# Opening the weight rooms' pool first, token 512 in other psum banks and on GpSimd, and a gate's Silu made earlier, in a fused Fourier and Hyena encoder layer

## The chip, the cores and the metric

The kernel runs on one core of a Trainium2 chip. The metric is device time in microseconds (us) of one launch, both sequences together. TensorE (PE) does the matmuls and the transposes; VectorE (DVE), ScalarE (ACT) and GpSimd (POOL) do elementwise work; SyncE (SP) and GpSimd's queue issue the transfers between HBM and the on-chip memory (SBUF). Matmul results land in psum banks.

## The reference, cut to what matters

Two sequences of 1024 tokens and 1024 channels go through one encoder layer, each as a batch of one. In the kernel they are batch row 0 and batch row 1.

```python
xn = rmsnorm(x, g_pre)
p = xn @ w_in                          # sections fv, fg, hv (three), hg, mg
fv, fg, hv, hg, mg = jnp.split(p, ...)

fz = fftn(fv by groups of 256 channels, axes=(tokens, channels), norm="ortho").real
y_f = (fz * silu(fg)) @ w_fourier_out

v, x1, x2 = jnp.split(short_conv(hv, w_short), 3, axis=-1)
z = v
for n, gate in enumerate((x1, x2)):
    z = gate * long_conv(z, filter spectrum n, hyena_d[n])
y_h = (z * silu(hg)) @ w_hyena_out

g_f, g_h = sigmoid(mg + b_merge) in two halves
out = (g_f * y_f + g_h * y_h) @ w_out
return x + rmsnorm(out, g_post)
```

The filters come from a small sine network: taps are made, weighted by an exponential decay, normalised, and transformed to spectra. In the kernel's numbering of w_in's sections 0 is fg, 1 to 3 are v, x1 and x2, 4 is hg, and 5 and 6 are mg. All values are fp32; every matmul operand is split in a high part `h` and a low part `l`, and three products are added (`mm3`).

## The kernel before

Four phases follow one another.

1. The Fourier phase, up to about 211 us with a tail to 250. Per 128 channels `xtile` (L334) transposes and scales x (`tpx`, tile `xg`), and forms sums and differences of tokens (`eo`, split to `eh` and `el`); token 512 has no partner and goes to a small tile `x5` (L360 and L361, two instructions of 128x2 for each k and batch row). The values fv (`pfv`) are computed in halves of 512 channels in the order (0,0), (0,1), (1,1), (1,0) of (batch row, half). In each half token 512 gets a product of its own, `pfx`, 16 matmuls into the psum tile `p5` (L410); its copy `x5t` enters the token stage (`stage`, psum `pse` and `pso`, copied to `sev`). A channel stage follows (`pP`, `pQ`, tiles `fPs`, `fPm`, `fA`, `fB`), and its result is stored to `d_fz` by GpSimd's queue. Psum has tags of a few banks each: "mm" of 4 banks, "T" of 2 and "X" of 2. The token stage uses "T" or "X".
2. `phase_main`, up to about 700 us. It makes 16 filter spectra: taps (psum `pft`, tiles `T`, `ex`, `acc`), their norm (`pn`), a butterfly and a transform (`pXf`, with the tables `cfw0` and `cfwd`). Between them stand 30 in-projections of gates for batch row 0 (`spill_gate`): sections 5 and 6 with eight tiles each, six tiles of section 4, and eight of section 0. A spilled gate goes to `d_g` in HBM. Section 0 gets its Silu there, as ps x (1 + tanh(ps / 2)) / 2, since tanh shares an ACT table with exp; the others are copied as they are.
3. The branches (`branches`), up to about 1640 us: short convolution, transform (`tph`, `pX`), product with the spectra and inverse transform (`pT`, tile `y`, cast to `yh`, remainder `yl`) for eight channel tiles, two orders and two batch rows. For section 4 of batch row 0 the first six tiles (`early`) load their gate from `d_g`, take Silu on ACT (L1021) and GpSimd multiplies; tiles 6 and 7 project the gate there.
4. The output blocks, up to 2408 us, in an order that is written out by hand.

An in-projection (`inproj`, L751) of a 128 x 1024 output tile is 48 matmuls of 128x512. Its weight comes in two halves. Each half needs a room of a high and a low tile: SP loads `wr`, ACT casts it to the high part (L773), ACT writes the negative of that to the low part (L774), and GpSimd's queue adds the original weight in HBM to it (an accumulating DMA, L775). Rooms go round in turns of four: two pairs `wh` and `wl`, then `draw` in the constant pool, then `draw2`, which has 4096 bytes per partition in the pool `m2`. The tile of the last two is called `whl`.

Up to the blocks the instruction order on each engine is not written by hand. A scheduler simulates the program with costs of its own and lets an instruction go when its operands, its tile and its psum bank are free in that simulation; each engine then runs its list strictly in order. A tile pool takes the address range that is free when it is opened, so the order of pools in `phase_main` decides which tiles of the Fourier phase a room or a table must wait for.

Of the kernel before, what the change touches and what calls it, by code (L numbers as in the profile page):

```python
# [12 lines left out]
AF = mybir.ActivationFunctionType  # L13
ALU = mybir.AluOpType
MUL, ADD, SUB = ALU.mult, ALU.add, ALU.subtract
# [146 lines left out]
class K:  # L162
# [171 lines left out]
    def xtile(self, b, k, px, fo):  # L334


        nc, a = self.nc, self.a
        if b == 0:
            xk = lambda m: self.xs[m][:, k * P:(k + 1) * P]
        else:  # L340
            xt = px.tile([P, 8, P], F32, tag="x", name=f"xk{b}_{k}", bufs=3)
            nc.sync.dma_start(xt, a[f"x{b}"].rearrange("(m p) c -> p m c", p=P)[:, :, k * P:(k + 1) * P])
            xk = lambda m: xt[:, m]
        xg = px.tile([P, L + 2], F32, tag="xg", name=f"xg{b}_{k}", bufs=2)
        nc.gpsimd.memset(xg[:, L:L + 2], 0.0)
        for n in range(2):
            tp = self.psum("mm", 4, "tpx") if b else self.psum("T", 2, "tpx")
            for q in range(4):
                m = 4 * n + q
                self.mm(tp[:, q * P:(q + 1) * P], xk(m), self.diag[:, m], True, True)  # L350
            nc.scalar.activation(xg[:, 512 * n:512 * n + 512], tp, AF.Copy, scale=self.gpre[:, k:k + 1])
        self.stored = nc.sync.dma_start(self.d_x[b][k], xg[:, 0:L])
        eo = px.tile([P, 2, 2, 256], F32, tag="eo", name="eo", bufs=2)
        fw = xg[:, 0:512].rearrange("p (a r) -> p r a", r=2)
        bw = xg[:, 1024:512:-1].rearrange("p (a r) -> p r a", r=2)
        self.add("dve", eo[:, 0], fw, bw)
        self.sub("pool" if b else "dve", eo[:, 1], fw, bw)
        self.split(fo["eh"][:, k], fo["el"][:, k], eo, "dve", "act")
        x5 = fo["x5"][:, k]
        mid = xg[:, 512:513].to_broadcast([P, 2])  # L360
        self.split(x5[:, b:b + 33:32], x5[:, 2 + b:35 + b:32], mid, "dve" if b else "pool", "dve" if b else "pool")  # L361


    def open_weights(self, pw):
# [26 lines left out]
    def fourier_half(self, b, half, W, fo, px, pf, begun={}):  # L391

        nc = self.nc
# [5 lines left out]
        for e, (W_, n, X_) in enumerate(((WE, 260, EE), (WO, 256, OO))):  # L399
            for m in range(4):  # L400
                p = begun.get((e, m))
                if p is None:
                    p = self.psum("mm", 4, f"pfv{e}")
                    for k in range(8):
                        self.pfv(p, e, m, k, W, fo)
                self.split(X_[0][:, m], X_[1][:, m], p[:, :n], "dve", "act")
                if e == (b + half == 0):

                    if m == 0:
                        p5 = self.psum("X", 2, "pfx")[0:36, :260]  # L410
                    for k in (2 * m, 2 * m + 1):
                        for i in range(2):
                            self.mm(p5, fo["x5"][:, k], WE[i][:, k], k + i == 0, k + i == 8)
# [390 lines left out]
    def spill_gate(self, b, sec, ct, ws):  # L804


        nc = self.nc
        ps = self.inproj(sec, ct, plain=b > 0)
        for n in range(2):
            s = slice(512 * n, 512 * n + 512)  # L810
            t = self.wp.tile([P, 512], F32, tag="gt", name="gt", bufs=3)
            if sec:
                nc.scalar.copy(t, ps[n])
            else:
                f = self.wp.tile([P, 512], F32, tag="gt", name="fz", bufs=3)
                nc.sync.dma_start(f, self.d_fz[b][ct][:, s])
                nc.scalar.activation(t, ps[n], AF.Tanh, scale=0.5)
                self.stt("dve", t, t, 1.0, ps[n], ADD, MUL)
                self.stt("dve", t, t, 0.5, f, MUL, MUL)
            nc.sync.dma_start(self.d_g[b][sec][ct][:, s], t)  # L820
# [92 lines left out]
    def phase_main(self, nct=8, nb=NB, nf=16):  # L913
        tc, nc, a = self.tc, self.nc, self.a
        with ExitStack() as es:
            pool = lambda n: es.enter_context(tc.tile_pool(name=n, bufs=1, reuse_waits="tile"))
            mf, wa, wb, mi = pool("mf"), pool("wa"), pool("wb"), pool("mi")
            self.stage2 = pool("m2")
            self.turn, self.unsaved = 3, []
            ws = Rooms(wa, wb)  # L920
            self.load_x(0, range(4))
            self.hid = ws.tile([P, L], F32R, tag="q", name="hid", bufs=2)
            hid = ws.tile([P, L], F32, tag="q", name="hidr", bufs=2)
            nc.sync.dma_start(hid, self.d_h)
            nc.scalar.copy(self.hid, hid)
            self.sub("dve", self.hid[64:128], hid[64:128], self.hid[64:128])
            taps = self.filter_taps(0, 0, ws)
            self.load_x(0, range(4, 8))
            self.cfw0 = mf.tile([P, 4 * P], F32, name="cfw0")
            self.cfwd = mf.tile([P, 2, 12 * P], F32R, name="cfwd")  # L930
            nc.sync.dma_start(self.cfw0, a["c_fw0"])
            nc.gpsimd.tensor_copy(self.cfwd[:, 0, 0:1], self.xl[4][:, 0:1])
            nc.gpsimd.dma_start(self.cfwd, a["c_fwd"])
            for t, n in ((self.th, "c_th"), (self.wsh, "w_short"), (self.bm, "b_merge")):
                nc.sync.dma_start(t, a[n])
            plain = [(5, c) for c in range(8)] + [(6, c) for c in range(8)] + [(4, c) for c in range(NH)]
            fill = sorted([((2 * c + 1) / len(plain), t) for c, t in enumerate(plain)]
                          + [((2 * c + 1) / max(NF, 1), (0, c)) for c in range(NF)])
            fill = [t for _, t in fill]
            for i in range(nf):  # L940
                nxt = self.filter_taps((i + 1) % 2, (i + 1) // 2, ws) if i + 1 < nf else None
                gates = fill[i * len(fill) // nf:(i + 1) * len(fill) // nf]
                if i < nf - 1:
                    self.filter_spectrum(i % 2, i // 2, taps, ws)
                for sec, c in gates:
                    self.spill_gate(0, sec, c, ws)
                if i == nf - 1:
                    first = [self.conv(1 + n, 0, ws, "vx"[n], 0, True) for n in range(2)]
                    self.filter_spectrum(i % 2, i // 2, taps, ws)
                taps = nxt  # L950
                if i == 4:
                    self.cinv = mi.tile([P, 2, INVW], F32R, name="cinv")
                if 4 <= i < 12:
                    w = slice((i - 4) * INVW // 8, (i - 3) * INVW // 8)
                    with tc.issue_after(self.added.ins):
                        nc.gpsimd.dma_start(self.cinv[:, :, w], a["c_inv"][:, :, w])
            self.branches(nb, nct, ws, *first)
# [33 lines left out]
    def branches(self, nb, nct, ws, v0, x0):  # L991
# [3 lines left out]
        tc, nc = self.tc, self.nc  # L995
# [8 lines left out]
        Z, X = {}, {}  # L1004
# [6 lines left out]
        def gates(i):  # L1011
            b, n, c = steps[i]
            x = self.conv(2 + n, c, ws, f"x{n + 1}", b)
            if n and b == 0:
                early = c < NH
                ps = None if early else self.inproj(4, c)
                for q in range(2):
                    sg = self.wp.tile([P, 512], F32, tag="gt", name="sg", bufs=3)
                    if early:
                        nc.sync.dma_start(sg, self.d_g[0][4][c][:, 512 * q:512 * q + 512])  # L1020
                    nc.scalar.activation(sg, sg if early else ps[q], AF.Silu)  # L1021
                    self.mul("pool", x[:, 512 * q:512 * q + 512], x[:, 512 * q:512 * q + 512], sg)
            X[i] = x
        B = self.conv_front(v0, ws)
# [509 lines left out]
```

## Time and profile before

| what | value |
|---|---|
| median of three runs | 2417.44 us (2414.99 to 2423.45) |
| the profiled execution | 2422.64 us, span 2420.8 us |
| PE busy | 2360.9 us, 98% of the span, 13006 matmuls |
| DVE busy | 1978.2 us, 82% |
| ACT busy | 1147.2 us, 47% |
| GpSimd busy | 460.4 us, 19% |
| moved by DMA | 499.37 MB |
| mean granted PE clock | 0.993 |

A row of a timeline has the start, the length of the whole group, engine, line, operation, output and input tiles, and shape; x16 are sixteen such instructions in a row. In brackets stands how long the engine idled before it and what it then got. L194 is the helper through which nearly all matmuls are issued and L181, L177, L173 and L171 are helpers for elementwise work, so groups are told apart by their tiles. Busy matmuls overlap: a 128x512 matmul is shown with about 0.39 us, though one can start every 0.23 us. A row of the waits has the engine with what it was to run, the releaser, and then the total, the count and the longest.

### The profile page before, as it was taken

To read this page: it belongs to the slowest core of one execution; us is meant where nothing else is said; L and a number is where in the kernel's file an instruction comes from. 1 tells how busy PE (TensorE), PEld (TensorE's weight loads), DVE (VectorE), ACT (ScalarE), POOL (GpSimd) and SP (SyncE) were. 2 spreads that over 40 slices of the span, in tenths; PEclk is the share of its full clock that TensorE was granted. 3 is DMA by queue.
4 is the path that set the end of the run, shared out by engine and by line. 5 is a ranking of instruction groups with operands and counts; after the bars stand their busy time and mean duration, and the time that the engine had idled before them with its cause. 6 is when DMAs were issued, how large, how long until landed. Compare 5 with 4: busy or idle time off the path is not lost. (4 is left out here: it accounts for less than half of the span.)

```text
span 2420.8 us, 37131 instructions
## 1 busy us (share of the span) xinstructions
PE 2360.9 (98%) x13006; PEld 2050.1 (85%) x13006; DVE 1978.2 (82%) x3744; ACT 1147.2 (47%) x2140; POOL 460.4 (19%) x595
## 2 busy tenths in 40 slices
PE   7999899999999999999999999999999999999998
PEld 6998788888888888888888888888878888888786
DVE  7786888888638999999899999997666687777787
ACT  6546666667544444444223222333344465656543
POOL 3331111111132232321034444310000000101000
PEclk9999999999999999999999999999999999999999
DMA  7737687787788777665365666553546688888744
GB/s 250 231 105 233 178 226 214 212 227 214 193 234 246 222 222 210 187 182 191 126 208 174 219 210 205 175 178 122 204 165 226 214 290 262 261 272 234 214 158 155
DMA packets 265426, 499.37 MB, mean 206 GB/s; under 512 B 26694, under 2 KB 92455, under 8 KB 265112
## 3 DMA queue, kind: packets, MB, share of 16 engines
q1 hardware_dynamic: 220092, 380.27, 47.9%
q0 software_dynamic: 44960, 116.72, 18.9%
q8 instruction: 102, 1.67, 0.3%
q14 instruction: 84, 0.69, 0.1%
q10 hardware_dynamic: 188, 0.02, 0.0%
HBM read 333.59 MB, written 167.51 MB: 207 GB/s over the span
## 5 line engine op out<-in xcount | busy, mean ns | idle before, releaser
L194 PE MATMUL pin<-xh,wh 128*128 128x512 f32 x1024 | 400.9, 392 | 0.3 <-DMA wh<-d_w 0.3
L194 PE MATMUL pin<-xl,wh 128*128 128x512 f32 x1024 | 401.1, 392 | 0.0
L194 PE MATMUL pin<-xh,wl 128*128 128x512 f32 x1024 | 399.8, 392 | 1.3 <-DMA wl<-d_w 1.3
L194 PE MATMUL pin<-xh,whl 128*128 128x512 f32 x896 | 291.2, 396 | 8.1 <-DMA whl<-in_w_in 4.5
L194 PEld LDWEIGHTS pin<-xh,wl 128*128 128x128 f32 x1024 | 192.7, 188 | 37.4 <-DMA wl<-d_w 1.7
L194 PEld LDWEIGHTS pin<-xh,wh 128*128 128x128 f32 x1024 | 192.8, 189 | 35.7 <-DMA wh<-d_w 0.8
L194 PEld LDWEIGHTS pin<-xl,wh 128*128 128x128 f32 x1024 | 192.7, 188 | 34.7
L194 PEld LDWEIGHTS pin<-xh,whl 128*128 128x128 f32 x896 | 167.2, 189 | 42.1 <-DMA whl<-in_w_in 5.2
L194 PE MATMUL pT<-cinv,yh 128*128 128x256 f32 x1024 | 192.9, 283 | 2.3 <-ACT yh L171 2.3
L194 PE MATMUL pin<-xl,whl 128*128 128x512 f32 x448 | 177.6, 397 | 0.0
L194 PEld LDWEIGHTS pT<-cinv,yh 128*128 128x128 f32 x1024 | 165.4, 191 | 12.5 <-ACT yh L171 2.8
L194 PE MATMUL pX<-bh,cfwd 128*128 128x256 f32 x768 | 159.4, 287 | 1.0 <-ACT bh L171 1.0
L181 DVE TENSOR_TENSOR t<-pX,k 128x1024 f32<-128x1024 f32 x128 | 155.3, 1213 | 3.8 <-PE pX L194 3.0
L171 ACT CAST yh<-y 128x512 fp32r<-128x512 f32 x128 | 79.3, 620 | 160.2 <-DVE y L181 122.6
L194 PE MATMUL pT<-cinv,yl 128*128 128x256 f32 x512 | 145.6, 284 | 0.0
L171 ACT CAST bh<-b 128x512 fp32r<-128x512 f32 x144 | 89.0, 619 | 100.5 <-DVE b L181 61.6
L194 PEld LDWEIGHTS pX<-bh,cfwd 128*128 128x128 f32 x768 | 126.1, 192 | 4.7 <-ACT bh L171 1.4
L181 POOL TENSOR_TENSOR draw<-draw 128x256 f32<-128x256 f32 x96 | 90.3, 940 | 114.1 <-DMA draw<-in_w_out 41.6
L194 PE MATMUL pX<-bl,cfwd 128*128 128x256 f32 x384 | 110.0, 286 | 1.2 <-DVE bl L181 1.2
L181 DVE TENSOR_TENSOR bl<-b,bh 128x512 fp32r<-128x512 f32 x144 | 100.0, 700 | 12.7 <-ACT bh L171 12.5
L181 DVE TENSOR_TENSOR yl<-y,yh 128x512 fp32r<-128x512 f32 x128 | 92.4, 722 | 13.9 <-ACT yh L171 13.7
L177 DVE SCALAR_TENSOR_TENSOR x<-pin,wsh,x 128x512 f32<-128x512 f32 (+1 forms) x128 | 90.3, 739 | 12.0 <-ACT x L795 11.9
(372 smaller groups left out, 6049.6 us busy)
## 6 DMA issues: line engine op xcount, KB each, us to landing
k<-d_k SPq DMA_DIRECT2D x128, 512.0 KB, 4.5
wr<-in_w_in SPq DMA_DIRECT2D x136, 256.0 KB, 3.5
d_g<-gt SPq DMA_DIRECT2D x92, 256.0 KB, 3.2
d_k<-kt SPq DMA_DIRECT2D x128, 128.0 KB, 3.7
d_k<-kt SPq DMA_DIRECT2D x64, 256.0 KB, 3.8
fz<-d_g SPq DMA_DIRECT2D x64, 256.0 KB, 5.2
wl<-in_w_in POOLq DMA_DIRECT2D x56, 256.0 KB, 5.3
whl<-in_w_in POOLq DMA_DIRECT2D x56, 256.0 KB, 5.5
```

What stands on the lines that cost most here:

```text
L171: self.rounded = nc.scalar.copy(h, src)
L177: self.nc.vector.scalar_tensor_tensor(out, a, s, b, op0=op0, op1=op1)
L181: return e.tensor_tensor(out, a, b, op=op)
L194: return self.nc.tensor.matmul(out, lhsT, rhs, start=start, stop=stop, skip_group_check=shared)
```

## The change

Four edits in one:

- In `xtile` the split of token 512 moves for batch row 1 too from DVE to GpSimd: 8 casts and 8 subtractions of 128x2.
- `pfx` takes a psum bank of tag "T" in the three halves whose `e` is 0, instead of "X".
- `spill_gate` makes Silu for section 4 as well: tanh in place of the copy, one DVE instruction (t + 1) x ps, one ACT multiplication by 0.5, for 12 half tiles. The branches then load the finished gate, and 12 ACT Silus go.
- `phase_main` opens the pool m2, in which `draw2` lies, first, and wa before mf. In the built programs `draw2` moves from an address that it shares with `sev`, `fPs` and `fPm` of the Fourier phase to one that it shares with `eh`; the table `cfwd` moves over `el`, `x5` and `x5t`.

```diff
-        self.split(x5[:, b:b + 33:32], x5[:, 2 + b:35 + b:32], mid, "dve" if b else "pool", "dve" if b else "pool")
+        self.split(x5[:, b:b + 33:32], x5[:, 2 + b:35 + b:32], mid, "pool", "pool")
...
-                        p5 = self.psum("X", 2, "pfx")[0:36, :260]
+                        p5 = self.psum("T" if e == 0 else "X", 2, "pfx")[0:36, :260]
...
-            if sec:
+            if sec == 4:
+                nc.scalar.activation(t, ps[n], AF.Tanh, scale=0.5)
+                self.stt("dve", t, t, 1.0, ps[n], ADD, MUL)
+                nc.scalar.mul(t, t, 0.5)
+            elif sec:
                 nc.scalar.copy(t, ps[n])
...
-            mf, wa, wb, mi = pool("mf"), pool("wa"), pool("wb"), pool("mi")
             self.stage2 = pool("m2")
+            wa, mf, wb, mi = pool("wa"), pool("mf"), pool("wb"), pool("mi")
...
                     if early:
                         nc.sync.dma_start(sg, self.d_g[0][4][c][:, 512 * q:512 * q + 512])
-                    nc.scalar.activation(sg, sg if early else ps[q], AF.Silu)
+                    else:
+                        nc.scalar.activation(sg, ps[q], AF.Silu)
                     self.mul("pool", x[:, 512 * q:512 * q + 512], x[:, 512 * q:512 * q + 512], sg)
```

The scheduler reorders all engines between about 85 and 700 us. The first 449 rows of PE's list are the same in both, and so are its last 6657; in the branches ACT's list differs by the missing Silus alone. Three places follow. Numbers behind a tile's name tell its copies apart.

ACT before, where the room draw2 (`whl_3590`) is first filled: behind the taps' exponentials.

```order
L655 ACTIVATE ex_3113<-T0_3099 128x512
L655 ACTIVATE ex_3124<-T1_3100 128x512
L171 CAST w3s_3362<-w3_3359 128x256
L652 ACTIVATE ex_3135<-dec_3096,vec_68 128x256 x2
L655 ACTIVATE ex_3135<-T1_3100 128x512
L773 CAST whl_3590<-wr_3591 128x512
L641 ACTIVATE dec_3365<-dec_3365 128x256
L774 ACTIVATE whl_3590<-whl_3590 128x512
```

ACT of the change, at the same room:

```order
L480 COPY fPs_2369<-pP_2357 128x256
L171 CAST oo0_2493<-pfv1_2674 128x256
L481 ACTIVATE fPm_2370<-pP_2357,vec_68 128x256
L171 CAST oo0_2493<-pfv1_2701 128x256
L773 CAST whl_3590<-wr_3591 128x512
L439 COPY sev_2753<-pse_2738 128x258
L774 ACTIVATE whl_3590<-whl_3590 128x512
L439 COPY sev_2778<-pse_2763 128x258
```

The room's cast has moved from the taps of the second filter to the end of the last half's `pfv` (`oo0` is the last tile split there), ahead of the first `sev`. GpSimd's queue of the change, from there on (`cfwd` stood ahead of `wl_3637` before):

```order
L775 DMA whl_3590<-in_w_in 128x512
L775 DMA wl_3637<-in_w_in 128x512
L775 DMA whl_3905<-in_w_in 128x512
L775 DMA wl_3668<-in_w_in 128x512
L491 DMA d_fz1_0_101<-fA_2833 128x1024
L492 DMA d_fz1_1_102<-fB_2834 128x1024
L775 DMA whl_3935<-in_w_in 128x512
L775 DMA wl_3974<-in_w_in 128x512
L936 COPY cfwd_3083<-xl0_4_3063 128x1
L937 DMA cfwd_3083<-in_c_fwd 128x3072
L491 DMA d_fz1_2_103<-fA_2901 128x1024
L492 DMA d_fz1_3_104<-fB_2902 128x1024
```

Six room fills have moved ahead of `cfwd`, and the room `wl_4005` comes behind these rows. The second place is ACT at token 512 of the last half, before:

```order
L171 CAST oo0_2493<-pfv1_2701 128x256
L925 CAST hid_2991<-hidr_2992 128x1024
L171 CAST w3s_2999<-w3_2996 128x256
L641 ACTIVATE dec_3002<-dec_3002 128x256
L416 CAST x5t_279<-pfx_2522 36x260
L652 ACT_TABLE_LOAD
L652 ACTIVATE ex_3009<-dec_3002,vec_68 128x256 x2
L652 ACTIVATE ex_3019<-dec_3002,vec_68 128x256 x2
L439 COPY sev_2753<-pse_2738 128x258
```

ACT of the change, at the same copy:

```order
L774 ACTIVATE wl_3292<-wh_3291 128x512
L773 CAST wh_3322<-wr_3324 128x512
L416 CAST x5t_279<-pfx_2522 36x260
L481 ACTIVATE fPm_2302<-pP_2289,vec_68 128x256
L774 ACTIVATE wl_3323<-wh_3322 128x512
L773 CAST whl_3560<-wr_3561 128x512
L171 CAST oo0_2493<-pfv1_2620 128x256
```

The copy `x5t` has moved ahead of all four casts of `oo0`, and the table load with the exponentials behind four copies to `sev`. The third place is ACT in the branches, at the gate of tile 5 of batch row 0, before:

```order
L171 CAST yh_11359<-y_11357 128x512
L1021 ACTIVATE sg_12235<-sg_12235 128x512
L884 COPY T0s_11338<-pT_11325 128x512
L773 CAST whl_12160<-wr_12161 128x512
L171 CAST yh_11398<-y_11396 128x512
```

The same place in the change:

```order
L171 CAST yh_11375<-y_11373 128x512
L888 COPY T0s_11354<-pT_11341 128x512
L773 CAST whl_12174<-wr_12175 128x512
L171 CAST yh_11414<-y_11412 128x512
```

Only the Silu is gone.

## The prediction

> **What bounds the kernel now.** I began with the page's first part, for the engine that is busiest, and then the waits of that engine (in all, times, longest), of which these rows lie where the edits do.
>
> ```profile
> PE 2360.9 (98%) x13006; PEld 2050.1 (85%) x13006; DVE 1978.2 (82%) x3744; ACT 1147.2 (47%) x2140; POOL 460.4 (19%) x595
> ...
> PE pin L194 <- DMA whl<-in_w_in: 4.5, 1, 4.5
> ...
> PE pin L194 <- ACT whl L773: 3.6, 1, 3.6
> ...
> PE tpx L194 <- DMA xk<-in_x: 2.6, 1, 2.6
> ...
> PE pT L194 <- ACT yh L171: 2.3, 1, 2.3
> ```
>
> TensorE (PE) is the bound: 2360.9 of 2420.8 us. An edit can therefore help only in the few places where PE stands still, or has just stood still and runs slowly. The stretches below hold the places that are touched, and two references.
>
> ```profile
> 105.00:137.00 32.00, 29.36 (x240) 28.89 (x239) 28.84 (x55) 22.40 (x36) 16.77 (x16) 0.95 0.76 255
> 195.00:215.00 20.00, 15.29 (x98) 13.31 (x98) 11.90 (x25) 11.51 (x21) 1.06 (x2) 0.91 0.87 312
> 248.00:271.00 23.00, 13.46 (x64) 10.81 (x63) 18.93 (x45) 12.55 (x25) 3.67 (x5) 0.78 0.53 140
> 300.00:660.00 360.00, 359.94 (x1982) 312.05 (x1981) 297.25 (x720) 242.03 (x524) 45.25 (x55) 1.00 0.79 216
> 560.00:700.00 140.00, 140.00 (x720) 119.48 (x719) 83.31 (x196) 76.87 (x153) 23.52 (x31) 1.00 0.77 210
> 924.00:990.00 66.00, 62.69 (x370) 54.94 (x370) 57.72 (x104) 26.60 (x46) 23.00 (x25) 1.00 0.66 190
> 2100.00:2160.00 60.00, 60.00 (x266) 49.70 (x265) 47.40 (x66) 37.36 (x59) 2.38 (x3) 1.00 0.76 248
> ```
>
> Columns: stretch, length, busy time of PE, weight load, DVE, ACT and GpSimd (POOL), then the granted clock. In 2100 to 2160 PE runs 266 matmuls without a gap, 0.226 us each (60.00 / 266): that is the pace against which losses are counted. PE idles 4.71 us in 195 to 215, 9.54 in 248 to 271 and 3.31 in 924 to 990, 17.6 us in all, and in the first two its clock drops. From 300 to 660, where the Silu work is added, it idles 0.06 us.
>
> **The weight rooms (pools opened in another order).** The largest hole:
>
> ```profile
> 252.16 0.74 PE L194 MATMUL pft<-w3s,hid 128*128 128x256 f32 x4 [1.40 <-DVE T L181]
> 256.51 0.79 PE L194 MATMUL pin<-xh,whl 128*128 128x512 f32 x1 [3.61 <-ACT whl L773]
> 257.10 0.63 PE L194 MATMUL pin<-xl,whl 128*128 128x512 f32 x1
> 257.53 0.63 PE L194 MATMUL pin<-xh,whl 128*128 128x512 f32 x1
> 263.11 1.22 PE L194 MATMUL pin<-xh,whl 128*128 128x512 f32 x2 [4.52 <-DMA whl<-in_w_in]
> 266.42 0.40 PE L194 MATMUL pin<-xl,whl 128*128 128x512 f32 x1
> ...
> 255.32 0.63 ACT L655 ACTIVATE ex<-T 128x512 f32<-128x512 f32 x1 [0.82 <-DVE T L181]
> 255.86 0.60 ACT L773 CAST whl<-wr 128x512 fp32r<-128x512 f32 x1
> 258.06 0.61 ACT L774 ACTIVATE whl<-whl 128x512 fp32r<-128x512 f32 x1
> ...
> 258.97 0.89 POOL L775 DMA_DIRECT2D whl<-in_w_in  x1 [6.50 <-ACT whl L774]
> ```
>
> The room draw2 is filled by a chain: cast (ACT, 255.86), negation (258.06), accumulating DMA (258.97), and PE gets the low part at 263.11. The cast stands behind the taps' exponentials in ACT's queue, which wait for DVE. In the changed order the same cast stands some fifty ACT rows earlier, among the last casts of pfv (around 200 us), its DMA too, so both waits should go. Not one instruction is added or removed. The place holds 1.40 + 3.61 + 4.52 = 9.5 us of idleness and a slow clock: 256.51 to 257.53 holds two spacings of 0.51 where 0.226 is the pace, and the eight matmuls from 263.11 to 266.42 took 3.31 us where 8 x 0.226 = 1.81 would do. That is 0.6 + 1.5 = 2.1 us of clock, 11.6 in all. I leave the wait for DVE's T (1.40), since the taps' own chain is not shortened: **10.2 us**, with bounds 3.6 (the cast's wait alone) and 11.6. What is late next: cfwd, the transform's table of 1.5 MB, which was issued ahead of all but three room fills,
>
> ```profile
> 220.25 0.53 POOL L933 DMA_DIRECT2D cfwd<-in_c_fwd  x1 [0.35 <-POOL cfwd L932]
> ```
>
> stands in the new order behind six room fills in GpSimd's queue, with two d_fz stores and the room wl_4005 behind it; that is a rival below.
>
> **Token 512 (its psum tag).** pfx is 16 small matmuls in either place, its copy one ACT instruction; nothing is added.
>
> ```profile
> 198.39 0.43 DVE L181 TENSOR_TENSOR fB<-pQ,fPm 128x258 f32<-128x258 f32 x1 [2.77 <-DMA d_fz<-fA]
> ...
> 197.66 0.87 PE L194 MATMUL pso<-seq,ee 128*128 128x258 f32 x6
> 199.66 0.62 PE L194 MATMUL pQ<-qp,chan 128*128 128x256 f32 x3 [1.12 <-DVE fB L177]
> 205.52 0.51 PE L194 MATMUL pse<-alt,x5t 128*128 128x258 f32 x2 [2.01 <-DVE x5t L181]
> 208.34 1.50 PE L194 MATMUL pse<-seq,ex 128*34 128x258 f32 x6 [1.58 <-ACT sev L439]
> ...
> 205.03 1.28 ACT L652 ACT_TABLE_LOAD   x1
> 206.32 1.70 ACT L652 ACTIVATE ex<-dec,vec 128x256 f32<-128x256 f32 x4
> 207.93 0.35 ACT L439 COPY sev<-pse 128x258 f32<-128x258 f32 x1
> ```
>
> pfx waited for an "X" bank until the channel stage gave one up, then the token stage waited for x5t (2.01), and sev stood behind a table load and four exponentials on ACT (1.58). With "T" banks pfx runs among the pfv matmuls, x5t is copied before the last pfv casts, and sev comes before the table load. Both waits go, 3.6 us; the 1.12 stays, because fB hangs on the landing of d_fz. The six matmuls behind the second wait took 1.50 where six like them took 0.87 at 197.66, and six more of the same kind follow them: 1.2 us of clock. **4.8 us**, bounds 2.0 (the x5t wait alone) and 5.9 (the 1.12 too).
>
> **Token 512 on GpSimd.** Eight pairs of 128x2 instructions leave DVE for GpSimd in the stretch 105 to 137. Batch row 0's pairs stand there already:
>
> ```profile
> L173 POOL CAST x<-xg x8: 186/200/4926, 25.5 to 56.5; 128x2 fp32r<-128x2 f32 x8
> L181 POOL TENSOR_TENSOR x<-xg,x x8: 194/320/1177, 25.7 to 56.8; 128x2 fp32r<-128x2 f32 x8
> ```
>
> By the medians a pair costs 0.52 us, eight 4.2; GpSimd is idle 32.00 - 16.77 = 15.2 us in that stretch. PE's one wait there is for an input DMA (xk, 2.6), which neither DVE nor this queue releases. **0 us**; bounds: a gain of 2.6 if all of PE's idleness there hung on DVE, and a loss of 34 if every pair took its maxima (8 x 6.1 = 49, less the 15.2 idle). I take the medians, since one held cast in eight makes the mean.
>
> **Silu in the spectra.** The 12 ACT Silus in the branches go; 12 DVE and 12 ACT instructions of these forms are added, and 12 tanh stand where 12 copies stood. The existing gates of section 0 already have such a tanh and such a DVE instruction:
>
> ```profile
> L817 ACT ACTIVATE gt<-pin 128x512 f32<-128x512 f32 x16 | 9.4, 590 | 4.1 <-PE pin L194 3.3 <-DVE gt L177 0.7
> L177 DVE SCALAR_TENSOR_TENSOR gt<-gt,pin 128x512 f32<-128x512 f32 x16 | 10.9, 679 | 15.0 <-ACT gt L817 15.0
> ```
>
> 12 x 0.68 = 8.1 us on DVE, and 12 x 0.61 = 7.3 on ACT, where a multiplication by a constant of that size is the row at 258.06 above; tanh costs 0.59, about what the copy did. Beside PE's unbroken 140 us, DVE has 140.00 - 83.31 = 56.7 us free in 560 to 700 and ACT 63: the matmuls hide them, **0 us**. Without that cover, DVE's 8.1 would be paid; that is the other bound. The psum banks of such a tile come free one DVE instruction (0.68) later, against 48 matmuls of 0.226 = 10.8 us for the tile that needs the next pair of banks. What goes away lies in 924 to 990:
>
> ```profile
> 979.41 0.68 DVE L181 TENSOR_TENSOR y<-t 128x512 f32<-128x512 f32 x1
> 985.79 0.63 ACT L1021 ACTIVATE sg<-sg 128x512 f32<-128x512 f32 x1 [9.99 <-DMA sg<-d_g]
> 987.31 0.62 ACT L171 CAST yh<-y 128x512 fp32r<-128x512 f32 x1
> 987.98 0.50 PE L194 MATMUL pT<-cinv,yh 128*128 128x256 f32 x2 [2.32 <-ACT yh L171]
> ```
>
> y was ready at 980.09, but its cast stood on ACT behind a Silu that waited for its gate's load, and PE stopped. GpSimd's multiply now takes that load itself, and ACT's queue is free. **3.3 us** (the idleness of the stretch), bounds 2.3 (this wait alone) and 7.2 (all by which yh was late, 987.31 - 980.09), if DVE, which has only 8.3 us free there, carried the rest of that lateness into later stretches. Next late is the multiply itself, which waits for the load on GpSimd, off PE's path until the gate is applied.
>
> **Sum.** 10.2 + 4.8 + 0 + 0 + 3.3 = 18.3 us. The profiled execution took 2422.64 us, of which the span is 2420.8 and 1.8 lies around it; it would become 2404.3. It is 5.2 above the median of the runs, 2417.44, so the median becomes **2399.1**. The places follow one another on the one bounding engine, and what stands behind them is written in the same order as before, so the gains add.
>
> **Rivals.**
> - *A new wait in GpSimd's DMA queue takes the place of the old one*, for cfwd or for wl_4005 behind it. For it: both stand behind stores that wait for DVE's fA, and a wait for one such load cost 4.52 idle and 1.5 of clock. Against it: PE has the matmuls of six more room fills (24 each, 5.4 us) ahead of the first that needs cfwd. Price: 6 back, 2405; twice, 2411.
> - *The room does not come earlier in time*, because its owner before, eh or another tile of the Fourier phase, is held to the end of pfv, and the gates catch up with it again. The 10.2 stay: 2409.3. Against it: the last pfv runs at 197 us, 60 before the cast of today.
> - *The slower side: GpSimd's small copies are held by DVE.* The row that speaks for it is the maximum of 4926 ns beside a median of 200. If each is held, the chain of eo, x5 and memset on GpSimd, which makes the next xk's tiles, runs 34 us over and PE with it: 2399 + 34 = 2433. From a pair of about 4.2 us ((15.2 + 18.3) / 8) the kernel is slower than before. Against it: one in eight was held, and the stretch of batch row 1 has DVE no fuller (28.84 of 32.00) than a few copies can find gaps in.
>
> The Trainium skill, "SBUF — State Buffer", section "Who interferes with whom", says that a DVE instruction with two SBUF inputs contends with a GpSimd instruction that reads SBUF, through a shared port pair held for the whole instruction. It speaks against this edit; the trace agrees in that single instructions are held (4926 against 200), not in that all are. By it alone the third rival would be likelier.
>
> **How the numbers follow.** This kernel's measurement tells a change from none at about 0.3%, 7.3 us: below 2410.2 is faster, above 2424.7 slower. Forecast, 2393 to 2403: 0.57. More than that (T's wait and the 1.12 go too, 3 us, and better packing): 0.07. A new wait in the queue, 2403 to 2411: 0.18, of which 0.02 beyond 2410.2. The room no earlier, about 2409: 0.09, half of it beyond. GpSimd held: 0.05, of which slower 0.04. The added DVE work unhidden with other gains missing, near 2415: 0.04, same. Faster 0.57 + 0.07 + 0.16 + 0.045, about 0.84; slower 0.04 and 0.01 for the unforeseen, 0.05; same 0.11. The range for 8 in 10 goes from 2390 (the upper bounds, 11.6 + 5.9 + 7.2 + 2.6 = 27.3) to 2410 (the room's gain missing).
>
> **What would show it.** The rooms: no PE wait for whl between 245 and 270, and a granted clock there near 1.00 instead of 0.78. Token 512: no wait for x5t or sev near 200; the wait for fB still there. Silu: no ACT wait for sg's load before the seventh tile, PE full in the stretch that was 924 to 990, and still full from 300 to 660. GpSimd: the casts of x5 keep a median of some 200 ns, and tpx waits no longer for eo or memset. I am wrong if a wait for wl or whl of over 3 us stands anywhere from 215 to 300, if PE idles over 3 us from 300 to 700, or if the stage from 100 to 145 grows.

## The result, and the profile after

The changed kernel took 2400.05 us (2397.50 to 2401.67, four runs) beside 2416.89 before (four runs): a ratio of 0.9916, 95% interval 0.9898 to 0.9933, 16.8 us less by the medians and 20.3 by the ratio. The forecast was 2399.1 us, 18.3 less. The total agrees, but its terms do not: the trace shows that near 200 us nothing was gained, and that between 211 and 270 more went than was forecast.

The first part of the page and the longest waits of PE, of the changed kernel:

```profile
PE 2355.1 (98%) x13006; PEld 2048.6 (85%) x13006; DVE 1976.7 (82%) x3740; ACT 1144.3 (48%) x2140; POOL 479.0 (20%) x611
...
PE tpx L194 <- DVE dg L332: 10.3, 2, 9.4
PE pQ L194 <- DVE fB L177: 5.0, 2, 4.5
...
PE tpx L194 <- DMA xk<-in_x: 0.6, 1, 0.6
```

The waits for whl and yh are gone, and so are those for x5t and sev near 200. A new one has come: pQ waits 4.5 us for fB, where it waited 1.12. A small one stands in an earlier half, where pfx now waits 1.02 us for sev at 90.49. The stretches, first of the changed kernel (columns as in the prediction, with the busy share of the 16 DMA engines and GB/s behind the clock; the fifth is the old 924 to 990, some 17 us earlier), then three of the kernel before that were not shown:

```profile
100.00:145.00 45.00, 41.73 (x348) 40.53 (x347) 35.76 (x62) 26.56 (x46) 27.31 (x36) 1.00 0.67 229
180.00:215.00 35.00, 30.50 (x232) 29.51 (x231) 19.27 (x51) 17.82 (x38) 5.69 (x8) 0.95 0.74 226
211.00:270.00 59.00, 59.00 (x312) 50.68 (x310) 44.02 (x86) 42.18 (x82) 9.15 (x13) 1.00 0.81 246
300.00:660.00 360.00, 360.00 (x1998) 313.50 (x1997) 304.46 (x735) 244.88 (x535) 46.52 (x58) 1.00 0.80 217
905.00:975.00 70.00, 70.00 (x417) 62.16 (x416) 67.79 (x123) 28.48 (x49) 25.68 (x27) 1.00 0.74 206
```

```profile
100.00:145.00 45.00, 42.36 (x348) 41.89 (x347) 36.94 (x76) 26.93 (x47) 17.86 (x18) 0.96 0.60 206
180.00:215.00 35.00, 30.29 (x224) 28.31 (x223) 21.12 (x54) 20.93 (x44) 4.80 (x7) 0.95 0.79 252
211.00:270.00 59.00, 49.46 (x254) 41.62 (x253) 43.58 (x94) 34.91 (x68) 8.11 (x12) 0.91 0.63 196
```

From 211 to 270 PE is now busy without a gap (59.00 of 59.00, before 49.46) at a clock of 1.00 (0.91). From 905 to 975 it is full too. From 180 to 215, where token 512's banks were to give 4.8 us, nothing has changed: 4.50 us idle against 4.71, the clock 0.95 in both. From 300 to 660, where twelve half tiles more of Silu are made, PE does not stop.

What happened near 200 is read from three queues of the changed kernel:

```profile
190.68 0.92 SPq L731 DMA_DIRECT2D xl<-d_x  x2
191.65 0.49 SPq L731 DMA_DIRECT2D xl<-d_x  x1
205.73 0.32 SPq L731 DMA_DIRECT2D xl<-d_x  x1
...
192.36 0.56 POOL L491 DMA_DIRECT2D d_fz<-fA  x1 [0.19 <-issue]
...
202.84 0.43 DVE L181 TENSOR_TENSOR fB<-pQ,fPm 128x258 f32<-128x258 f32 x1 [6.86 <-DMA d_fz<-fA]
...
204.11 0.69 PE L194 MATMUL pQ<-qp,chan 128*128 128x256 f32 x3 [4.50 <-DVE fB L177]
205.45 1.49 PE L194 MATMUL pse<-seq,ee 128*128 128x258 f32 x6
208.12 0.90 PE L194 MATMUL pse<-seq,ee 128*128 128x258 f32 x6
```

And the same loads and the same store before, with the time for which one of SP's loads of xl waited for pfx:

```profile
197.26 0.33 SPq L924 DMA_DIRECT2D hidr<-d_h  x1
200.55 7.14 SPq L731 DMA_DIRECT2D xl<-d_x  x8
...
191.16 0.56 POOL L491 DMA_DIRECT2D d_fz<-fA  x1
...
SPq L731 <- PE pfx L194: 1.5, 1, 1.5
```

The store d_fz was issued 1.2 us later than before (192.36 against 191.16 for its first), but the tile of fA that it empties, and that fB takes next, came free 4.5 us later (202.84 against 198.39). Just before the store, SP now issues three loads of xl, of 512 KB each, from 190.68 to 191.65; before, they began at 200.55, behind hidr. My theory after the result: pfx, once it runs among the pfv matmuls, is done with its operands some 17 us earlier (it starts at 182.71 and not at 200.48); tiles of xl lie in addresses that it reads, as the wait of 1.5 us for pfx indicates; the scheduler lets their loads go first, 10 us earlier than before; they share the DMA engines with the store (from 188 to 206 SP's queue takes 40.1% of the 16 engines and GpSimd's 39.0%), and the store is what the channel stage waits for.

### The profile page after: what moved, and what is told of

Read it like the earlier page. It is cut to its first block, busy times and chain, and to the rows that moved or that the text cites. A ratio compares the mean times of both kernels' runs of the same rounds, so it can differ in the third digit from the quotient of the medians.

```text
span 2399.7 us, 37150 instructions
## 1 busy us (share of the span) xinstructions
PE 2355.1 (98%) x13006; PEld 2048.6 (85%) x13006; DVE 1976.7 (82%) x3740; ACT 1144.3 (48%) x2140; POOL 479.0 (20%) x611
## 5 line engine op out<-in xcount | busy, mean ns | idle before, releaser
L181 POOL TENSOR_TENSOR draw<-draw 128x256 f32<-128x256 f32 x96 | 99.0, 1031 | 116.7 <-DMA draw<-d_sh 39.4
L194 PEld LDWEIGHTS pT<-cinv,yl 128*128 128x128 f32 x512 | 98.0, 191 | 1.9
```

The lines of the kernel that those rows point to most:

```text
L181: return e.tensor_tensor(out, a, b, op=op)
L194: return self.nc.tensor.matmul(out, lhsT, rhs, start=start, stop=stop, skip_group_check=shared)
```

## The experiments

Eight kernels were timed, in two groups of four. The median of before was 2418.45 us beside the first group and 2421.82 beside the second.

**The pools alone.**

```diff
-            mf, wa, wb, mi = pool("mf"), pool("wa"), pool("wb"), pool("mi")
             self.stage2 = pool("m2")
+            wa, mf, wb, mi = pool("wa"), pool("mf"), pool("wb"), pool("mi")
```

> The kernel before with the pools in the new order and nothing else. Theory (the room's price stood too low, and the new wait for fB comes from token 512's banks, which free the room of pfv's weights early and so let the loads of xl run ahead of the d_fz stores): no PE wait for whl at 249 to 270, 13 us gained there, the wait of pQ for fB stays near 1.1 us, the waits for x5t and sev near 200 stay; time about 13 us below before (2404). Rival (the new order of pools itself moves the loads of xl): pQ waits 4.5 us for fB here too and the gain is 9 to 10 us (2407).

Measured: 2406.14 us, ratio 0.9946 (0.9931 to 0.9962), 13.1 us less by the ratio. Stretches of this kernel, then its SP queue and DVE near 200:

```profile
248.00:271.00 23.00, 23.00 (x118) 19.57 (x118) 17.07 (x37) 12.68 (x27) 5.33 (x8) 1.00 0.90 272
300.00:660.00 360.00, 357.39 (x1980) 309.88 (x1979) 300.48 (x730) 240.54 (x526) 44.92 (x55) 1.00 0.78 214
...
206.12 6.30 SPq L731 DMA_DIRECT2D xl<-d_x  x8
...
203.16 0.43 DVE L181 TENSOR_TENSOR fB<-pQ,fPm 128x258 f32<-128x258 f32 x1 [3.77 <-DMA d_fz<-fA]
```

The hole is gone, and the loads of xl keep their late place, so the pools did not move them. pQ's wait was 2.1 us, between the two theories' figures. Of the two waits that were expected to stay near 200, sev's did (1.49) and x5t's did not. PE idled 2.6 us from 300 to 660, most of it at two places (for kt 0.8, for acc 1.2): a part of the lead was given back in the spectra in this order; with all four edits PE idled 0.00 and 0.33 us there in the two profiles.

**The T banks alone.**

```diff
-                        p5 = self.psum("X", 2, "pfx")[0:36, :260]
+                        p5 = self.psum("T" if e == 0 else "X", 2, "pfx")[0:36, :260]
```

> The kernel before with pfx in a T bank and nothing else. Theory: the waits for x5t (2.0) and sev (1.6) go, three loads of xl are issued near 191 us instead of 200, d_fz lands later, pQ waits 4 to 5 us for fB instead of 1.1; the stretch from 195 to 215 gains nothing and the time is within 2 us of before, while the hole at 249 to 270 stays. Rival (the banks alone are worth what was forecast): 4.8 us below before (2412), pQ's wait for fB near 1.1.

Measured: 2418.43 us, ratio 1.0003 (0.9993 to 1.0013): nothing, where 4.8 us had been forecast for this edit. SP, DVE and PE of this kernel:

```profile
190.75 15.81 SPq L731 DMA_DIRECT2D xl<-d_x  x4
...
203.03 0.43 DVE L181 TENSOR_TENSOR fB<-pQ,fPm 128x258 f32<-128x258 f32 x1 [6.61 <-DMA d_fz<-fA]
...
204.30 1.01 PE L194 MATMUL pQ<-qp,chan 128*128 128x256 f32 x3 [4.25 <-DVE fB L177]
```

This edit alone brings the loads of xl from 200.6 to 190.8 and pQ's wait from 1.12 to 4.25, and no other wait is left there. What it saves at x5t and sev it pays at fB.

**Silu alone.**

```diff
-            if sec:
+            if sec == 4:
+                nc.scalar.activation(t, ps[n], AF.Tanh, scale=0.5)
+                self.stt("dve", t, t, 1.0, ps[n], ADD, MUL)
+                nc.scalar.mul(t, t, 0.5)
+            elif sec:
                 nc.scalar.copy(t, ps[n])
...
-                    nc.scalar.activation(sg, sg if early else ps[q], AF.Silu)
+                    else:
+                        nc.scalar.activation(sg, ps[q], AF.Silu)
```

> The kernel before with Silu made in the spectra and nothing else. Theory: the waits at 933 and 985 go, nothing is paid from 560 to 700; 3.3 to 3.9 us below before (2413). Rival (the added DVE and ACT work costs up to 8.1 us in the spectra): 2413 to 2421, with idle PE from 560 to 700.

Measured: 2412.46 us, ratio 0.9971 (0.9959 to 0.9983), 7.0 us less, between 4.1 and 9.9. Stretches of this kernel:

```profile
924.00:990.00 66.00, 66.00 (x391) 58.45 (x390) 64.47 (x116) 27.79 (x48) 22.38 (x25) 1.00 0.68 202
560.00:700.00 140.00, 140.00 (x719) 119.44 (x719) 91.94 (x212) 80.77 (x165) 24.34 (x32) 1.00 0.77 213
```

The added work is hidden: DVE rises by 8.6 us in the second stretch (91.94 against 83.31; 8.1 were worked out) and PE is full. The 3.31 us of idle PE at 924 to 990 are gone. The rest, at least 0.8 us by the interval and 3.7 by its middle, I could not place. The two profiled executions differ by 8.2 us, and a good part of that lies from 1500 to 1600, where tph's wait for T1s was 4.00 us with a clock of 0.97 before and 3.12 with 1.00 here. But the same wait was 1.01 with the T banks alone and 0.80 with token 512 alone on GpSimd, which gained nothing, so it can't be credited to this edit.

**Token 512 on GpSimd alone.**

```diff
-        ... mid, "dve" if b else "pool", "dve" if b else "pool")
+        ... mid, "pool", "pool")
```

> The kernel before with token 512 of batch row 1 on GpSimd and nothing else. Theory: nothing within 1 us (2416 to 2418); the wait for xk near 117 us, 2.6 before, may change by its own course of transfers. Rival (DVE, relieved, lets the stage from 100 to 145 run faster): 2 to 3 us below before, the stage shorter by as much. Rival (GpSimd is held by DVE): casts of over 3 us in most of the eight and the stage longer.

Measured: 2418.98 us, ratio 1.0005 (0.9995 to 1.0015): nothing. The casts from 100 to 145 in this kernel, and then in the changed one:

```profile
L173 POOL CAST x<-xg x8: 178/416/647, 109.4 to 135.6; 128x2 fp32r<-128x2 f32 x8
```

```profile
L173 POOL CAST x<-xg x8: 177/652/660, 110.4 to 139.7; 128x2 fp32r<-128x2 f32 x8
```

The three figures behind the colon are the shortest, the median and the longest in ns. The median rose from 200 in batch row 0 to 416 and 652, so the sign in the prediction, a median of some 200, failed. But no cast of batch row 1 took more than 0.66 us, in the changed kernel beside a DVE that was busy for 35.76 of 45.00 us, and nothing like the 4.9 us of one cast of batch row 0 came. This edit alone also reordered the stage near 200 (PE idles 3.17 us from 180 to 215 instead of 4.71, at a clock of 0.90 instead of 0.95), and that gained nothing either.

**The changed kernel again**, as a reference for the three that follow. No edit.

> The changed kernel itself, once more, beside the three that follow: ratio to before 0.992 (2400), pQ waits 4 to 5 us for fB near 200.

Measured: 2400.26 us, ratio 0.9913 (0.9895 to 0.9930). The new wait was 5.56 us in this profile.

**The first four loads of xl behind hidr.** SP's queue takes hidr first, as it did before the change; nothing else is written differently.

```diff
-            self.load_x(0, range(4))
             self.hid = ws.tile([P, L], F32R, tag="q", name="hid", bufs=2)
             hid = ws.tile([P, L], F32, tag="q", name="hidr", bufs=2)
-            nc.sync.dma_start(hid, self.d_h)
+            first = nc.sync.dma_start(hid, self.d_h)
+            with tc.issue_after(first.ins):
+                self.load_x(0, range(4))
```

> The changed kernel with the first four loads of xl queued on SP behind the load of hidr, which waits for a room until about 197 us. Theory (loads of xl, issued near 191, keep the d_fz store of 192 from landing): xl is issued after 197, DVE's fB is held 2 to 3.5 us by d_fz instead of 6.9, pQ waits 1 to 2 us instead of 4.5, and the time is 3 to 4 us below the changed kernel, if the xl that come later do not make the in-projections at 212 wait. Rival (the store lands late for another reason, such as three accumulating DMAs ahead of it in its own queue): pQ's wait stays at 4 us or more, the time does not change.

Measured: 2395.72 us (2393.50 to 2398.59, five runs), ratio to before 0.9898 (0.9880 to 0.9915); the mean of its runs is 4.4 us below that of the changed kernel's six on the same chip, with about 3 us of uncertainty. By the medians it is 4.5. SP, GpSimd's queue, DVE and PE of this kernel, and two stretches:

```profile
200.47 0.33 SPq L927 DMA_DIRECT2D hidr<-d_h  x1
200.85 2.70 SPq L731 DMA_DIRECT2D xl<-d_x  x4
...
193.00 0.57 POOL L491 DMA_DIRECT2D d_fz<-fA  x1 [0.19 <-issue]
...
200.77 0.43 DVE L181 TENSOR_TENSOR fB<-pQ,fPm 128x258 f32<-128x258 f32 x1 [3.96 <-DMA d_fz<-fA]
...
202.04 0.63 PE L194 MATMUL pQ<-qp,chan 128*128 128x256 f32 x3 [1.60 <-DVE fB L177]
...
180.00:215.00 35.00, 32.88 (x254) 31.17 (x254) 23.37 (x58) 19.69 (x41) 5.73 (x8) 1.00 0.78 230
300.00:660.00 360.00, 358.13 (x1972) 310.50 (x1971) 299.70 (x726) 242.99 (x530) 46.17 (x57) 1.00 0.80 215
```

The store is issued no earlier (193.00 against 192.36), and still its tile comes free 2.1 us earlier, 7.8 us after the issue instead of 10.5. pQ waits 1.60 instead of 4.50, and the clock in 180 to 215 is 1.00 instead of 0.95. The rival, that accumulating DMAs ahead in the store's own queue make it late, would have left the wait as it was; they stand there unchanged. They may explain what is left; the last experiment bears on that. From 300 to 660 PE now idles 1.87 us where the changed kernel had none, so a part of the lead is given back in the spectra. The rows show that the loads of xl make the wait; they do not account for the whole 4.4 us in the same way. In the profiled pair tph's wait for T1s near 1500 also fell, from 3.44 to 0.50 us, and no run shows whether that hangs on the loads. This version is the fastest measured, below both kernels.

**All loads of xl behind the first taps' loads**, the order that they had before the change.

```diff
-            self.load_x(0, range(4))
...
             taps = self.filter_taps(0, 0, ws)
-            self.load_x(0, range(4, 8))
+            with tc.issue_after(self.last_load.ins):
+                self.load_x(0)
```

Here `last_load` is the load of `db` in `filter_taps`.

> The changed kernel with all eight loads of xl behind the first taps' five loads on SP, the order that they had before. Theory: as with hidr_first, pQ's wait 1 to 2 us, x5t's and sev's waits still gone, 3 to 5 us below the changed kernel (2396). Rival of the same sign as a loss: xl then arrives too late for the in-projections at 212, PE waits there for xh or xl by 3 us or more, and nothing is won.

Measured: 2402.92 us, ratio 0.9925 (0.9908 to 0.9941), not faster than the changed kernel. SP and PE of this kernel:

```profile
202.76 6.93 SPq L731 DMA_DIRECT2D xl<-d_x  x8
...
200.97 0.63 PE L194 MATMUL pQ<-qp,chan 128*128 128x256 f32 x3 [0.88 <-DVE fB L177]
209.05 0.98 PE L194 MATMUL pso<-seq,oo 128*128 128x258 f32 x6 [1.56 <-DVE sst L445]
212.36 0.77 PE L194 MATMUL pin<-xh,wh 128*128 128x512 f32 x2 [2.33 <-ACT xh L171]
```

pQ's wait fell below 1 us, as the theory had it, but the gain that it forecast did not come. The rival named beforehand did: with two microseconds more of lateness of xl (202.76 against 200.85) the first in-projection waited 2.33 us for xh. Of the three times at which these loads were tried, 190.7 and 202.8 each cost a wait of over 2 us, and 200.9 one of 0.47 (for xl).

**All but the T banks.**

```diff
-                        p5 = self.psum("T" if e == 0 else "X", 2, "pfx")[0:36, :260]
+                        p5 = self.psum("X", 2, "pfx")[0:36, :260]
```

> The changed kernel with pfx back in an X bank. Theory (what the T banks give at x5t and sev they take at fB): the waits for x5t and sev are back, pQ's wait for fB is 1 to 2 us, the time within 2 us of the changed kernel. Rival (the banks are worth what was forecast): 4.8 us above it.

Measured: 2402.32 us, ratio 0.9929 (0.9911 to 0.9947); 2 us above the changed kernel on the same chip, the two intervals overlapping. PE and the store of this kernel, the last row with the time from the store's issue to its landing (2.9 us):

```profile
202.07 0.63 PE L194 MATMUL pQ<-qp,chan 128*128 128x256 f32 x3 [1.46 <-DVE fB L177]
204.74 3.17 PE L194 MATMUL pfx<-we,x 128*36 128x260 f32 x16 [1.67 <-ACT fPm L481]
209.79 0.51 PE L194 MATMUL pse<-alt,x5t 128*128 128x258 f32 x2 [0.71 <-DVE x5t L181]
...
196.43 0.57 POOL L491 DMA_DIRECT2D d_fz<-fA  x1 [4.98 <-DVE fA L177]
...
d_fz<-fA POOLq DMA_DIRECT2D x1, 512.0 KB, 2.9
```

Without the T banks the same stretch has three small waits of 3.84 us together in place of one of 4.50. sev's wait, which I had expected back, did not come; pfx waited instead. The edit is worth nothing alone and about 2 us here (3.3 by the means), which the noise does not tell from none. The kernel with hidr first lies 6.6 us below this one by the medians, but it differs from it in more than the banks, so what the banks are worth with the loads held back stays an estimate.

The store says more about the rival of two experiments ago. Here, and with token 512 on GpSimd alone, it is issued 5.8 and 5.7 us behind the last accumulating DMA of GpSimd's queue instead of 0.9 to 1.2, it lands after 2.9 us in both, and fB does not wait for it. So the 7.1 us that the store took before the change were long already, and the accumulating DMAs just ahead of it are the likely cause of some 4 of them. The loads of xl add 3 to 5 on top. No run moves the accumulating DMAs alone, so the first part is not shown as the second is.

## Why the prediction was right, and where it was not

The forecast of 2399.1 us and the range held, and the sign was as forecast. That the sum came out so near is luck: 4.8 us forecast for token 512's banks did not come, and the middles of two other terms measured 2.9 and 3.7 us more than forecast.

- **The weight rooms: right in mechanism, probably too small.** 10.2 us were forecast, 13.1 (9.2 to 16.7) measured with the pools alone, so the time alone does not refute 10.2. The trace does refute one step, "I leave the wait for DVE's T (1.40)": between 211 and 270 PE of the changed kernel has no gap left at all, and with the pools alone there is none from 248 to 271. My reading is that with the rooms filled there is other work to run while T is made. The upper bound of that step, 11.6, was nearer.
- **Token 512's banks: wrong.** The step that failed is "the 1.12 stays, because fB hangs on the landing of d_fz". Both waits went as forecast, and x5t was copied early as the order had shown, but the wait for fB grew to 4.50 us. I had costed the 16 matmuls that move and not what they release: the addresses that they read, and through them SP's loads of xl, which then meet the store. The 4.8 us were measured as nothing (1.0003). That the cause is the loads and not the banks is shown by the kernel that keeps the banks and holds the loads behind hidr: there the wait is 1.60 us and the kernel 4.4 us faster, and over eight profiles the store's tile came free after 10.5 to 12.0 us with the loads ahead and after 7.1 to 8.2 without.
- **Token 512 on GpSimd: right at nothing.** DVE busy in 100 to 145 fell by 1.2 us and POOL's rose by 9.5, and PE idled 3.27 us there instead of 2.64, at a clock of 1.00 instead of 0.96; it ran 348 matmuls in both, so the stage did not grow. The 9.5 are more than twice the 4.2 that I had worked out from the medians; GpSimd had room for them.
- **Silu: right in mechanism, too small.** 3.3 us forecast, 7.0 (4.1 to 9.9) measured alone. The part that the profile shows is the 3.31; where the rest comes from is open. Nothing was paid in the spectra.
- **The sum.** The four edits alone measured -13.1, +0.7, -7.0 and +1.2 us, -18.2 together; all four at once -20.3 and -21.1 in the two comparisons, each with some 4 us of uncertainty. Within that the gains add.

The rivals. GpSimd's queue: no wait for cfwd or wl_4005 came, and the lead was kept to 660 us. A room that comes no earlier: not so; its cast stood near 206 us and not at 255.86. It came later than the 200 I had read from the order, at least in part because the channel stage ahead of it was itself late. GpSimd held by DVE: no cast of the eight took over 0.66 us. By the rule of the Trainium skill that I had set beside that rival ("SBUF — State Buffer", section "Who interferes with whom") it was a danger; in this kernel the eight casts were slowed two- to threefold by the medians, none was held for long, and no run shows what slowed them. A rival that I did not list is the one that happened in part: a new wait on the other side of an edit, in the one stretch where I had kept an old wait as a constant.

## What to carry to other kernels

When work moves earlier, ask what its last read releases, and which queue is waiting for that address: a prefetch that starts early was not free here, because a store on the critical path shared the DMA engines with it. A wait that stays "because it hangs on a transfer" has a price of its own that other transfers set, so its row must be read again in the changed order, in every queue. And a sum that agrees does not show its terms: only the edits one at a time did.

## What the runs showed of the hardware

The time from a 512 KB store's issue until its tile was free hung on what was issued around it. With three 512 KB loads of xl just ahead it took 10.5, 10.6 and 12.0 us in three kernels; without them 7.1 to 8.2 in five (7.8 with hidr first). In the two kernels in which the accumulating DMAs stood 5.7 us or more ahead of it, it landed after 2.9.

The clock did not fall after every wait. With one wait of 4.50 us the next six matmuls of 128x258 took 1.49 us and only those of 208.12 were back at 0.90; with a wait of 1.60 in the kernel with hidr first the granted clock in the stretch stayed at 1.00. But before the change three waits of 1.12, 2.01 and 1.58 us within 9 us cost a clock of 0.91 from 195 to 215. And in the kernel with the pools alone one wait of 2.12 us was enough: behind it the 16 matmuls of pfx took 3.26 us, where they took 2.07 before, and the clock was 0.66 from 205 to 210.

```profile
204.43 0.63 PE L194 MATMUL pQ<-qp,chan 128*128 128x256 f32 x3 [2.12 <-DVE fB L177]
205.27 3.26 PE L194 MATMUL pfx<-we,x 128*36 128x260 f32 x16
...
205.00:210.00 5.00, 5.00 (x29) 4.39 (x28) 4.22 (x10) 4.33 (x8) 1.95 (x3) 0.66 0.74 98
```

The Trainium skill ("TensorE: Matmul & The Clock Gate", "Part 1: The HAM clock gate") puts the limit at an idle window of about 3.4 us. The 4.50 and the 1.60 agree with that; the 2.12 and the three waits close together do not, and here the measurement decides.
